# Splitting the output-projection weights on ScalarE and GpSimd, and one gating product on VectorE

## The chip, the cores and the metric

The kernel runs on one core of one Trainium2 chip. The metric is the device time of one execution in microseconds (us). A difference is measured by running the kernel before and the changed kernel on the same chip.

## What is computed

Two groups of tokens (1024 and 512, together 1536 rows of 1024 values) go through two layers that share their weights.

```python
def attn_retention_layer(x, g, w_in, qk_gain, ret_decay, w_out):
    z = rmsnorm(x, g) @ w_in
    ...
    mixed = jnp.concatenate([jax.nn.silu(ga) * oa, jax.nn.silu(gb) * ob], axis=-1)
    return x + mixed @ w_out

def windowed_layer(x, g, w_in, sink, rel_bias, w_out):
    z = rmsnorm(x, g) @ w_in
    ...
    return x + (jax.nn.silu(gate) * o) @ w_out
```

The first layer mixes tokens by dense attention (mixer A) and by retention (mixer B), the second by windowed attention (mixer C). In both, a gate multiplies the branch output, and the product goes through an output projection of 1024x1024 (w_out). A last RMSNorm follows.

## The kernel before, in words

**Products in two parts.** The matrix products run on TensorE with operands rounded to the type fp32r. To keep precision each operand is split into a high part (the rounded value) and a low part (what the rounding lost), and each product is the sum of three: high by high, low by high, high by low. For a weight tile the split is in `load_w`: a raw tile `wraw` of 128x512 (256 KB, two buffers) is fetched by a DMA on SP's queue; line 139 writes the high part on GpSimd; line 140 writes the low part, raw minus high, on GpSimd or, where the argument `lo` says so, on VectorE. The split tile `w` has four buffers. A raw buffer is free again when the low part is done, a `w` buffer when TensorE has used it.

**Tokens** are worked on in three groups t of 512 (four blocks of 128), in the order t = 2, 0, 1.

**The feature-major output projection**, `out_proj_fm`, is run for t = 2 and then t = 0 in each layer. It loops over four column chunks c; for each it calls `load_w`, which yields four `w` tiles; each tile serves 12 matmuls of 128x512 (output tile `pso`). So there are 16 `w` tiles for a group and 32 for a layer. In the first layer (weights `woab`) both parts are made on GpSimd; in the second (weights `woc`) `lo` is `nc.vector`. Line 281 adds the residual, line 283 squares the result on ScalarE, line 285 adds the square to `acc` on GpSimd.

**Where it runs.** `out_proj_fm` is a generator. Its pieces fill TensorE's queue between the pieces of attention (`pipeline`, classes `Fill` and `FillC`): while the attention of group t = 0 is computed, the projection of t = 2 runs, and so on. For t = 1 a token-major projection, `out_proj`, closes each layer; it has its own calls of `load_w`, which the change leaves alone.

**Attention around it.** Scores `s` (or `sc`) come from TensorE; VectorE reduces their maximum; ScalarE takes the exponential (line 839, or 1045) into `e` (or `ec`); GpSimd scales that by the reciprocal of the sum (line 107); TensorE transposes it to `pte`; ScalarE writes the high part `eh` (line 111) and VectorE the low part `el` (line 112); TensorE accumulates `po`. `Back.evac` adds the two halves of `po` on VectorE into `oT` (line 702).

**Gating.** For most heads `oT` is written out, and `mix_fm` later loads it with its gate, multiplies on GpSimd (line 262, tile `mo`) and splits the product into `xh` on ScalarE and `xl` on VectorE. For the last heads of groups 1 and 0 in the first layer, and of group 1 in the second, `Back.mix` does this directly: line 713 multiplies `oT` by the gate `gq` on GpSimd, and `split` makes `xh` and `xl`. That is 12 products of 128x256 in all.

**What sets the order.** Nothing is ordered by hand on an engine: the framework's scheduler (`schedule_with_timeline_sim=True`) plays the program on its own model of the engines and fixes the order of every engine's queue by it. At run time each engine works through its queue in that order and waits where an operand or a buffer isn't ready. So an instruction that moves to another engine also changes the order of the others near it.

Of the kernel before, what the change touches and what calls it, by code (L numbers as in the profile page):

```python
# [10 lines left out]
AF = mybir.ActivationFunctionType  # L11
ALU = mybir.AluOpType
# [6 lines left out]
KT = D // P  # L19
# [17 lines left out]
def trunk_kernel(ctx, tc, x, xT, wab, woab, wc, woc, gT, qkg, ret, sink, relb, fng,  # L37
                 ropeA, ropeB, dist, kdist, qdist, onehot, wmask, out_p0, out_p1, out_s):
    nc = tc.nc
# [13 lines left out]
    def buf(tag, name, n=None, dt=F32):  # L53
        t = wk.tile([P, SIZE[tag]], dt, tag=tag, name=name, bufs=BUFS[tag])
        return t if n is None else t[:, :n]

    def ps_s(name):
        return pp.tile([P, 512], F32, tag="s", name=name, bufs=5)
# [6 lines left out]
    def ps_p(name, use="fill"):  # L65
        free = ring[use]
        ring["i"] = next(i % 3 for i in range(ring["i"] + 1, ring["i"] + 4) if i % 3 in free)
        return pp.tile([P, 512], F32, tag=f"pj{ring['i']}", name=name, bufs=1)
# [58 lines left out]
        new_x(k, t)  # L127
        split(X["h", k, t], X["l", k, t], src, scale, pool)

    def load_w(arr, c, tag, lo=None, hook=None, ks=range(KT), raws=None):  # L130
        ts = {}
        for i in (k // 2 for k in ks[::2]):
            if raws is None:
                raw = wp.tile([P, 2 * CW], F32, tag="wraw", name="wraw", bufs=2)
                dma(out=raw, in_=arr[c, :, 2 * i:2 * i + 2, :].rearrange("p k n -> p (k n)"))
            else:
                raw = raws[i]
            w = wp.tile([P, 2, 2 * CW], F32R, tag=tag, name=tag, bufs=4)
            nc.gpsimd.tensor_scalar(w[:, 0, :], raw, 1.0, 1.0, ALU.mult, ALU.mult)  # L139
            (lo or nc.gpsimd).tensor_tensor(w[:, 1, :], raw, w[:, 0, :].bitcast(F32), ALU.subtract)  # L140
            ts[i] = w
            if hook is not None:
                hook(i)

        def get(s, k, a=0, n=CW):
            o = (k % 2) * CW + a
            return ts[k // 2][:, s, o:o + n]
        return get
# [18 lines left out]
    def proj_fm_k(ps, w, a, t, k, ks=range(KT)):  # L167
        mm(ps, w(0, k, a, P), X["h", k, t], k == ks[0], False)
        mm(ps, w(0, k, a, P), X["l", k, t], False, False)
        mm(ps, w(1, k, a, P), X["h", k, t], False, k == ks[-1])  # L170
# [82 lines left out]
    def stage(name):  # L253
        s = wp.tile([P, 2, 2 * CW], F32R, tag="wg", name=name, bufs=4)
        return s[:, 0, :].bitcast(F32), s[:, 1, :].bitcast(F32)
# [7 lines left out]
            split_x(o, k, t, 0.5)  # L263
            yield

    def out_proj_fm(t, warr, ks, res, dst, finish, prev, lo):
        acc = buf("T", "acc")
        for c in range(4):
            w = load_w(warr, c, "w", lo, None, ks)
            for a in range(2):  # L270
                k = 2 * c + a
                y, sq = stage("y")
                dma(out=y, in_=res(k))
                ps = ps_p("pso")
                for kk in ks:
                    proj_fm_k(ps, w, a * P, t, kk, ks)
                    if kk != ks[-1]:
                        yield
                for side in ahead[:1] + (prev or []):
                    next(side, None)  # L280
                nc.vector.tensor_tensor(y, ps, y, ALU.add)
                dma(out=dst[k][t], in_=y)
                nc.scalar.activation(sq if k else acc, y, AF.Square)
                if k:
                    nc.gpsimd.tensor_tensor(acc, acc, sq, ALU.add)
                yield
        dg, one = stage("dg")
        nc.gpsimd.memset(one[:, :P], 1.0)
        ps = ps_s("ssq")
        for j in range(GB):  # L290
            mm(ps[:, j:j + 1], acc[:, j * P:(j + 1) * P], one[:, 0:1], True, True)
        r = rstd_of(ps[:, :GB], D, GB)
        ps = ps_s("R")
        for j in range(GB):
            nc.vector.tensor_scalar(dg[:, j * P:(j + 1) * P], ident, r[:, j:j + 1], None, ALU.mult)
            mm(ps[:, j * P:(j + 1) * P], one[:, :P], dg[:, j * P:(j + 1) * P], True, True)
        rb = buf("T", "rb")
        nc.scalar.activation(rb, ps, AF.Copy)
        yield

        def fin():
            for k in range(KT):
                y = stage("yn")[0] if prev is None else buf("Q", "yn")
                dma(out=y, in_=dst[k][t])
                finish(t, k, y, rb)
                yield
        if prev is None:
            late.append(fin())
        else:
            yield from fin()  # L310

    late, ahead = [], []

    def drain(gens):
        while gens:
            for _ in gens.pop():
                pass
# [35 lines left out]
    x1T_d, x2T_d = scratch("x1T"), scratch("x2T")  # L353
# [36 lines left out]
    raws, xts = [], []  # L390
# [267 lines left out]
    for h in range(4):  # L658
        w = ws[h]
# [9 lines left out]
    class Back:  # L669
# [38 lines left out]
        def mix(self, oT):  # L708
            g = buf("Q", "gq", 256).rearrange("p (a q) -> p a q", a=2)
            sl = slice(self.j * P, (self.j + 1) * P)  # L710
            for a in range(2):
                dma(out=g[:, a, :], in_=self.gd[self.k0 + a][self.t][:, sl])
            nc.gpsimd.tensor_tensor(oT, oT, g, ALU.mult)
            for a in range(2):
                k = self.k0 + a
                if self.j == 0:
                    new_x(k, self.t)
                split(X["h", k, self.t][:, sl], X["l", k, self.t][:, sl], oT[:, a, :], 0.5)
# [140 lines left out]
    def hook_a(u):  # L859
        g, b = u  # L860
        if g == 1 and b in (BLOCKS[GB], BLOCKS[2 * GB]):
            t = 2 if b == BLOCKS[GB] else 0
            if t == 2:
                late.clear()
                fill.rest()
                fill.rate = 2.00
            drain(ahead)
            if t:
                drain([mix_fm(t, KS_A, o_ab, g_ab)])
            ahead.append(mix_fm(0 if t else 1, KS_A[:6], o_ab, g_ab))  # L870
            fill.gens.append(out_proj_fm(t, woab, KS_A, lambda k: xT[k][:, t * 512:(t + 1) * 512], x1T_d, fin_fm,
                                         None if t else late, None))

    rq1 = buf("S4", "tab").rearrange("p (f b d) -> p f b d", f=2, b=8)
    dma(out=rq1, in_=tabq_d)
# [117 lines left out]
    fillc = FillC()  # L993
# [69 lines left out]
    KS_C = tuple(range(KT))  # L1063

    def hook_c(u):
        c, b = u
        if c == 3 and b in (BLOCKS[GB], BLOCKS[2 * GB]):
            t = 2 if b == BLOCKS[GB] else 0
            for _ in fillc.gates:
                pass  # L1070
            if t == 2:
                late.clear()
            drain(ahead)
            drain([mix_fm(t, KS_C if t else KS_C[6:], o_c, g_c)])
            ahead.append(mix_fm(0 if t else 1, KS_C[:6], o_c, g_c))
            fillc.more.append(out_proj_fm(t, woc, KS_C, lambda k: x1T_d[k][t], x2T_d, fin_out, None if t else late, nc.vector))

    pipeline([(c, b) for c in range(4) for b in BLOCKS], prep_c, front_c, BUFS["E"] - 4,
             lambda kb, n: 4 if kb == n - 1 else 0, lambda n: 3.5, fillc, hook_c)
# [108 lines left out]
```

## Time and profile before

| | us |
|---|---|
| median of 3 runs (lowest to highest) | 1510.15 (1509.29 to 1511.72) |
| the profiled execution | 1511.78 |
| its span, first to last instruction | 1509.9 |
| TensorE busy in the span (PE) | 1447.9 (96%) |
| VectorE busy (DVE) | 1051.6 (70%) |
| GpSimd busy (POOL) | 810.6 (54%) |
| ScalarE busy (ACT) | 717.7 (48%) |

How to read it: PE is TensorE's matmul side and PEld its weight loads, DVE is VectorE, ACT ScalarE, POOL GpSimd, SP the engine that issues most DMAs. The busy time of an engine says how full it was over the span, not whether it held up the end. PEclk, or the granted clock, is the share of TensorE's full 2.4 GHz that it was given. In a list of instructions in order of time, a bracket tells how long the engine had stood idle before the row, and which instruction ended that wait.

### The profile page before, as it was taken

The numbers are of one execution on the slowest core, as the hardware profiler recorded it, in microseconds if no ns is written. First come the engines' busy times: TensorE is split into PE (matmuls) and PEld (weight loads), VectorE is DVE, ScalarE is ACT, GpSimd is POOL, SyncE is SP. The second block draws the span as 40 slices with busy tenths as digits, with TensorE's granted clock in tenths as the row PEclk, the third lists the DMA queues.
The fourth block names the chain that finished last, engine by engine and source line by source line (L and its number), as shares of the span: only waits on it lengthen the run. The fifth ranks groups of instructions, "written<-read, shape, count | busy, mean of one in ns | idle before, by whom it ended". The sixth has DMA issues, their size and how long they took to land.

```text
span 1509.9 us, 26043 instructions
## 1 busy us (share of the span) xinstructions
PE 1447.9 (96%) x8734; PEld 1266.1 (84%) x8734; DVE 1051.6 (70%) x2431; ACT 717.7 (48%) x1770; POOL 810.6 (54%) x1044
## 2 busy tenths in 40 slices
PE   8989999989999999989998999999999999998987
PEld 8989999977888888767777998888888888776777
DVE  7455867686676667887978237687777767889574
ACT  5632222354555555645653245566555556545102
POOL 7554654474645475887887423442622522567442
PEclk9999999999999999999999999999999999999999
DMA  9631212326212143643664231221212211567872
GB/s 327 204 122 48 77 54 71 99 74 189 74 50 66 60 117 115 208 129 108 191 211 147 78 109 45 61 77 46 75 47 87 70 46 53 168 202 274 267 235 107
DMA packets 139638, 180.79 MB, mean 120 GB/s; under 512 B 38320, under 2 KB 66992, under 8 KB 139504
## 3 DMA queue, kind: packets, MB, share of 16 engines
q1 hardware_dynamic: 137344, 173.61, 36.6%
q0 software_dynamic: 2016, 5.51, 1.3%
q8 instruction: 69, 1.13, 0.3%
q14 instruction: 65, 0.53, 0.1%
q10 hardware_dynamic: 144, 0.01, 0.0%
HBM read 127.92 MB, written 55.35 MB: 121 GB/s over the span
## 4 chain that ended last, share of the span: by engine, by line
PE 69%; DVE 10%; DMA 6%; POOL 4%; issue 4%; ACT 1%; SPq 0%; POOLq 0%; DVEq 0%; ACTq 0%
PE psg L89 17%; PE psq L89 10%; PE po L89 8%; PE psb L89 8%; PE pso L89 6%; PE pte L173 6%; PE s L89 4%; PE sc L89 3%; PE pskv L89 2%; DVE xl L118 2%; DVE w L140 1%; DVE el L112 1%; DVE nm L831 1%; DMA wraw<-in_woc 1%; PE ptq L173 1%
## 5 line engine op out<-in xcount | busy, mean ns | idle before, releaser
L89 PE MATMUL psg<-xh,wg 128*128 128x512 f32 x768 | 264.0, 401 | 0.2 <-POOL wg L140 0.2
L112 DVE TENSOR_TENSOR el<-pte,eh 128x512 fp32r<-128x512 f32 x288 | 196.4, 684 | 57.4 <-ACT eh L111 33.7
L107 POOL TENSOR_SCALAR ec<-ec,rl 128x384 f32<-128x384 f32 (+1 forms) x192 | 108.5, 578 | 233.9 <-DVE rl L1050 82.2
L111 ACT ACTIVATE eh<-pte 128x512 fp32r<-128x512 f32 x288 | 169.6, 595 | 115.0 <-PE po L89 62.9
L89 PE MATMUL pso<-xh,w 128*128 128x512 f32 x512 | 179.1, 408 | 10.5 <-POOL w L139 4.9
L89 PEld LDWEIGHTS psg<-xh,wg 128*128 128x128 f32 x768 | 143.9, 189 | 29.2 <-POOL e L107 0.9
L107 POOL TENSOR_SCALAR e<-e,rl 128x512 f32<-128x512 f32 x160 | 114.6, 727 | 91.9 <-DVE rl L842 33.9
L89 PE MATMUL psg<-xl,wg 128*128 128x512 f32 x384 | 151.0, 393 | 0.0
L1045 ACT ACTIVATE ec<-ec,nm 128x384 f32<-128x384 f32 (+1 forms) x192 | 109.5, 572 | 81.0 <-DVE nm L1043 76.0
L839 ACT ACTIVATE e<-s,nm 128x512 f32<-128x512 f32 x160 | 108.8, 686 | 70.8 <-DVE nm L836 52.5
L139 POOL TENSOR_SCALAR w<-wraw 128x512 fp32r<-128x512 f32 x116 | 80.3, 694 | 102.4 <-PE pskv L89 32.2
L831 DVE TENSOR_REDUCE nm<-s 128x1 f32<-128x512 f32 x160 | 107.7, 682 | 36.6 <-PE s L89 36.2
L89 PE MATMUL psq<-xh,w 128*128 128x512 f32 x384 | 130.0, 397 | 0.0
L89 PEld LDWEIGHTS pso<-xh,w 128*128 128x128 f32 x512 | 96.6, 191 | 34.1 <-POOL w L139 7.0
L1039 DVE CUSTOM_DVE_ANT_0 ec<-sc,bias,sink_s 128x384 f32<-128x384 f32 (+1 forms) x192 | 105.2, 568 | 21.4 <-PE sc L89 18.2
L89 PE MATMUL pso<-xl,w 128*128 128x512 f32 x256 | 102.1, 399 | 1.7 <-DVE xl L118 1.7
L173 PE MATMUL pte<-ident,e 128*128 128x128 f32 x640 | 95.5, 274 | 1.0 <-ACT e L839 0.6
L173 PEld LDWEIGHTS pte<-ident,e 128*128 128x128 f32 x640 | 78.5, 141 | 19.2 <-ACT e L839 2.2
L140 POOL TENSOR_TENSOR w<-wraw,w 128x512 fp32r<-128x512 f32 x68 | 91.4, 1347 | 1.9
L89 PEld LDWEIGHTS psg<-xl,wg 128*128 128x128 f32 x384 | 72.5, 189 | 13.1
L89 PEld LDWEIGHTS psq<-xh,w 128*128 128x128 f32 x384 | 71.9, 188 | 13.6
L173 PE MATMUL pte<-ident,ec 128*128 128x128 f32 x512 | 78.5, 273 | 1.3 <-POOL ec L107 1.1
(227 smaller groups left out, 3941.1 us busy)
## 6 DMA issues: line engine op xcount, KB each, us to landing
wraw<-in_woab SPq DMA_DIRECT2D x48, 256.0 KB, 3.4
wraw<-in_woc SPq DMA_DIRECT2D x48, 256.0 KB, 4.1
wraw<-in_wab SPq DMA_DIRECT2D x44, 256.0 KB, 3.5
wraw<-in_wc SPq DMA_DIRECT2D x36, 256.0 KB, 3.2
xt<-in_xT SPq DMA_DIRECT2D x24, 256.0 KB, 5.3
xb<-in_x SPq DMA_DIRECT2D x24, 256.0 KB, 5.1
qd<-qd SPq DMA_DIRECT2D x48, 128.0 KB, 2.9
gab<-gz SPq DMA_DIRECT2D x24, 256.0 KB, 2.0
```

The source lines that it names most:

```text
L89: i = nc.tensor.matmul(ps, lhsT=lhsT, rhs=rhs, start=start, stop=stop)
L107: nc.gpsimd.tensor_scalar(o, i, s, 1.0, ALU.mult, ALU.mult)
L111: nc.scalar.activation(hi, src, AF.Copy)
L112: nc.vector.tensor_tensor(lo, src, hi.bitcast(F32), ALU.subtract)
L118: nc.vector.scalar_tensor_tensor(lo, src, scale, hi.bitcast(F32), ALU.mult, ALU.subtract)
L139: nc.gpsimd.tensor_scalar(w[:, 0, :], raw, 1.0, 1.0, ALU.mult, ALU.mult)
L140: (lo or nc.gpsimd).tensor_tensor(w[:, 1, :], raw, w[:, 0, :].bitcast(F32), ALU.subtract)
L173: return nc.tensor.transpose(o, i, ident)
L831: nc.vector.tensor_reduce(nm2[:, c:c + 1] if nh == 2 else nm[:, h:h + 1], s, AX.X, ALU.max, negate=True)
L839: nc.scalar.activation(eh[c], ss[c], AF.Exp, bias=nm[:, h:h + 1], accum_out=l[:, h, c:c + 1])
L1039: nc.vector.tensor_tensor_reduce(es[h][:, :nk], s, bias[h][:, bo:bo + nk], 1.0, sink_s[:, 4 * c + h:4 * c + h + 1], ALU.add, ALU.max, mx[: ...
L1045: nc.scalar.activation(es[a][:, :nk], es[a][:, :nk], AF.Exp, bias=nm[:, a:a + 1], accum_out=l[:, a:a + 1])
```

## The change

In the feature-major output projection of both layers the high part of a weight tile is made by ScalarE (a copy that rounds), and the low part by GpSimd. In the second layer the low part so moves from VectorE to GpSimd; in the first it stays there. The direct gating product moves from GpSimd to VectorE. In number: 64 high parts go from GpSimd to ScalarE, 32 low parts from VectorE to GpSimd, 12 products from GpSimd to VectorE. DMAs, buffers and matmuls stay as they are.

```diff
-    def load_w(arr, c, tag, lo=None, hook=None, ks=range(KT), raws=None):
+    def load_w(arr, c, tag, lo=None, hook=None, ks=range(KT), raws=None, act=False):
...
-            nc.gpsimd.tensor_scalar(w[:, 0, :], raw, 1.0, 1.0, ALU.mult, ALU.mult)
+            if act:
+                nc.scalar.activation(w[:, 0, :], raw, AF.Copy)
+            else:
+                nc.gpsimd.tensor_scalar(w[:, 0, :], raw, 1.0, 1.0, ALU.mult, ALU.mult)
             (lo or nc.gpsimd).tensor_tensor(w[:, 1, :], raw, w[:, 0, :].bitcast(F32), ALU.subtract)
...
-    def out_proj_fm(t, warr, ks, res, dst, finish, prev, lo):
+    def out_proj_fm(t, warr, ks, res, dst, finish, prev):
...
-            w = load_w(warr, c, "w", lo, None, ks)
+            w = load_w(warr, c, "w", None, None, ks, None, True)
...
-            nc.gpsimd.tensor_tensor(oT, oT, g, ALU.mult)
+            nc.vector.tensor_tensor(oT, oT, g, ALU.mult)
...
-                                         None if t else late, None))
+                                         None if t else late))
...
-            fillc.more.append(out_proj_fm(t, woc, KS_C, lambda k: x1T_d[k][t], x2T_d, fin_out, None if t else late, nc.vector))
+            fillc.more.append(out_proj_fm(t, woc, KS_C, lambda k: x1T_d[k][t], x2T_d, fin_out, None if t else late))
```

The scheduler gives every queue a new order in two stretches, the ones in which `out_proj_fm` runs; the order elsewhere stays. (In the changed file, lines from 141 on lie three further down, and line 140 is the new ScalarE copy.)

The first place is ScalarE's queue in the first layer, around the first direct gating product (`oT_8017`; `w_83..` are weight tiles of the second chunk of t = 2, `y_8061` a residual sum). Before:

```order
L283 ACTIVATE y_8061<-y_8061 128x512
L111 ACTIVATE eh_8037<-pte_8032 128x512
L117 ACTIVATE xh50_8296<-mo_8292 128x512
L117 ACTIVATE xh20_8024<-oT_8017 128x128
L117 ACTIVATE xh30_8028<-oT_8017 128x128
L111 ACTIVATE eh_8078<-pte_8073 128x512
L839 ACTIVATE e_8109,l_7876<-s_8100,nm_7874 128x512
```

After:

```order
L117 ACTIVATE xh50_8296<-mo_8292 128x512
L140 ACTIVATE w_8330<-wraw_8328 128x512
L140 ACTIVATE w_8335<-wraw_8333 128x512
L117 ACTIVATE xh20_8024<-oT_8017 128x128
L117 ACTIVATE xh30_8028<-oT_8017 128x128
L140 ACTIVATE w_8340<-wraw_8338 128x512
L111 ACTIVATE eh_8078<-pte_8073 128x512
L286 ACTIVATE y_8196<-y_8196 128x512
L842 ACTIVATE e_8109,l_7876<-s_8100,nm_7874 128x512
```

Three high parts of weights now stand between and around the splits of the gated product, ahead of the next `eh` and exponentials.

The second place is GpSimd's queue in the second layer, in the projection of t = 0 after the last attention block (`w_1735.` and `w_1736.` are tiles of its third chunk, `acc_17134` is the running sum of squares). Before, with the low parts elsewhere:

```order
L139 TENSOR_SCALAR w_17350<-wraw_17348 128x512
L139 TENSOR_SCALAR w_17355<-wraw_17353 128x512
L139 TENSOR_SCALAR w_17360<-wraw_17358 128x512
L285 TENSOR_TENSOR acc_17134<-acc_17134,y_17278 128x512
L285 TENSOR_TENSOR acc_17134<-acc_17134,y_17313 128x512
L139 TENSOR_SCALAR w_17365<-wraw_17363 128x512
```

After, these are the low parts:

```order
L143 TENSOR_TENSOR w_17350<-wraw_17348,w_17350 128x512
L288 TENSOR_TENSOR acc_17134<-acc_17134,y_17278 128x512
L143 TENSOR_TENSOR w_17355<-wraw_17353,w_17355 128x512
L288 TENSOR_TENSOR acc_17134<-acc_17134,y_17313 128x512
L143 TENSOR_TENSOR w_17360<-wraw_17358,w_17360 128x512
L143 TENSOR_TENSOR w_17365<-wraw_17363,w_17365 128x512
```

Each of the two sums of squares now stands ahead of the next low part, where it stood behind three high parts.

## Rows read from the trace of the kernel before

**Rows 1.** Busy us by stretch: stretch, length, PE, PEld, DVE, ACT, POOL, clock, DMA share, GB/s

```profile
600.00:790.00 190.00, 179.85 (x902) 143.14 (x901) 155.80 (x286) 108.58 (x243) 157.91 (x165) 0.99 0.56 173
...
1303.00:1403.00 100.00, 89.39 (x424) 70.72 (x423) 89.85 (x198) 51.76 (x130) 73.28 (x79) 0.98 0.73 241
1403.00:1450.00 47.00, 41.13 (x172) 31.48 (x170) 25.90 (x34) 5.53 (x9) 18.05 (x21) 0.96 0.81 268
```

**Rows 2.** PE in order of time, 640 to 680 us, where it stood idle

```profile
646.29 0.50 PE L89 MATMUL po<-eh,av 128*128 128x512 f32 x1 [1.39 <-ACT eh L111]
649.19 0.50 PE L89 MATMUL s<-ak,qh 128*128 128x512 f32 x1 [2.40 <-ACT e L839]
...
674.35 0.50 PE L89 MATMUL s<-ak,qh 128*128 128x512 f32 x1 [0.82 <-ACT e L839]
```

**Rows 3.** All engines in order of time, 638 to 650 us, around the first product

```profile
638.72 0.84 DVE L702 TENSOR_TENSOR oT<-po,olo 64x256 f32<-64x256 f32 x2
...
644.49 0.72 POOL L713 TENSOR_TENSOR oT<-oT,gq 128x256 f32<-128x256 f32 x1
...
645.24 0.51 ACT L117 ACTIVATE xh<-oT 128x128 fp32r<-128x128 f32 x2 [3.77 <-POOL oT L713]
```

**Rows 4.** Busy time by stretch of 10 us after that stall

```profile
640.00:650.00 10.00, 6.20 (x26) 4.43 (x25) 6.35 (x10) 3.26 (x9) 9.90 (x11) 1.00 0.36 113
650.00:660.00 10.00, 10.00 (x48) 8.29 (x47) 7.94 (x16) 5.91 (x13) 7.44 (x9) 0.83 0.72 194
```

**Rows 5.** Waits in 600 to 790 us: total us, times, longest

```profile
ACT xh L117 <- POOL oT L713: 9.2, 5, 3.8
...
POOL w L139 <- PE pso L89: 4.4, 2, 2.5
...
POOL w L139 <- DMA wraw<-in_woab: 1.2, 2, 0.9
```

**Rows 6.** Groups of instructions of the whole span: count, busy us, mean ns

```profile
L140 POOL TENSOR_TENSOR w<-wraw,w 128x512 fp32r<-128x512 f32 x68 | 91.4, 1347 | 1.9
...
L117 ACT ACTIVATE xh<-mo 128x512 fp32r<-128x512 f32 x42 | 26.2, 627 | 37.6 <-POOL mo L262 37.5
...
L345 DVE TENSOR_TENSOR xr<-pso,xr 128x256 f32<-128x256 f32 x32 | 13.1, 416 | 22.2 <-PE pso L89 22.2
...
L713 POOL TENSOR_TENSOR oT<-oT,gq 128x256 f32<-128x256 f32 x12 | 10.2, 847 | 2.9 <-DVE oT L702 2.9
```

**Rows 7.** PE in order of time, 1310 to 1360 us, where it stood idle

```profile
1317.36 0.47 PE L89 MATMUL pso<-xh,w 128*128 128x512 f32 x1 [1.98 <-DVE oT L702]
...
1331.12 0.50 PE L89 MATMUL po<-el,cv 128*128 128x512 f32 x1 [1.12 <-DVE el L112]
...
1333.06 0.69 PE L89 MATMUL sc<-ch,qs 128*128 128x384 f32 x1 [1.09 <-DVE el L112]
...
1351.60 0.47 PE L89 MATMUL po<-eh,cv 128*128 128x512 f32 x1 [1.13 <-DVE oT L702]
```

**Rows 8.** Groups of instructions, 1303 to 1403 us

```profile
L140 DVE TENSOR_TENSOR w<-wraw,w 128x512 fp32r<-128x512 f32 x20 | 18.4, 927 | 3.3 <-POOL w L139 3.3
...
L139 POOL TENSOR_SCALAR w<-wraw 128x512 fp32r<-128x512 f32 x20 | 14.9, 746 | 4.6 <-DMA wraw<-in_woc 4.4
...
L1049 DVE TENSOR_TENSOR l<-l,se 128x2 f32<-128x2 f32 x14 | 6.6, 473 | 0.9 <-ACT se L1048 0.9
```

**Rows 9.** Groups of instructions, 1403 to 1450 us

```profile
L89 PE MATMUL pso<-xh,w 128*128 128x512 f32 x106 | 35.7, 411 | 5.6 <-POOL w L139 4.9 <-DVE w L140 0.6
...
L140 DVE TENSOR_TENSOR w<-wraw,w 128x512 fp32r<-128x512 f32 x13 | 13.2, 1016 | 17.9 <-POOL w L139 17.9
...
L139 POOL TENSOR_SCALAR w<-wraw 128x512 fp32r<-128x512 f32 x13 | 8.6, 659 | 25.3 <-DMA wraw<-in_woc 25.3
L285 POOL TENSOR_TENSOR acc<-acc,y 128x512 f32<-128x512 f32 x5 | 6.9, 1386 | 1.2 <-ACT y L283 1.2
```

**Rows 10.** DMAs of raw weight tiles, 1403 to 1450 us

```profile
DMA to landing us min/median/max: 3.4/4.4/7.1
```

## The prediction

> **What bounds the kernel now.** I read the share of busy time first, then the busy time by stretch, then, inside the stretches that the change touches, TensorE's idle times, the waits, and the groups of instructions. TensorE is busy for 1447.9 of 1509.9 us, so at most 62 us of the span is idle, and only those parts of it that lie where the projection runs can be moved. Those are three stretches: 600 to 790 us (first layer), 1303 to 1403 us (second layer, t = 2) and 1403 to 1450 us (second layer, t = 0). The reader is to subtract TensorE's busy time from each length [rows 1]: 190 - 179.85 = 10.15 us idle, 100 - 89.39 = 10.61 us, 47 - 41.13 = 5.87 us. These 26.6 us are all that the change can win, apart from the clock.
>
> Each stretch has its own limit. In the first layer the largest stall is 1.39 + 2.40 us, where TensorE waits for ScalarE's `eh` and then its exponential `e` [rows 2]. ScalarE wasn't slow: VectorE had finished `oT` at 638.72 + 0.84 = 639.56, GpSimd came to the gating product only at 644.49, and ScalarE stood idle 3.77 us in front of the split `xh` with the exponentials queued behind it [rows 3]. GpSimd was busy for 9.90 of those 10 us [rows 4]. So a GpSimd queue holds up ScalarE and through it TensorE. After the stall the granted clock was 0.83 for 10 us, between the levels 1.2 and 2.4 GHz [rows 4].
>
> In the second layer at t = 2 VectorE is the engine behind the stalls: it is busy for 89.85 of 100 us [rows 1], and the stalls of over 1 us named to it between 1310 and 1360 us are 1.98 + 1.12 + 1.09 + 1.13 = 5.32 us [rows 7]. Its instructions there contain waiting: a sum of 128x2 elements takes 473 ns, half of what a low part of 128x512 takes (927 ns) [rows 8]. At t = 0 attention is over and the weights bound: of TensorE's 5.6 us of idle time before `pso`, 4.9 us ends with GpSimd's high part, and GpSimd itself waited 25.3 us for raw tiles, so it was not full but late data was [rows 9]. A raw buffer's round is landing 4.4 us [rows 10], high part 0.66, low part 1.02 [rows 9]: 6.1 us for two tiles in two buffers.
>
> **The change part by part.** Prices: a high part on ScalarE isn't in the trace. The nearest row, ScalarE's rounding copy `xh<-mo` of the same shape, takes 627 ns; GpSimd's 659 to 746 ns bounds it from above [rows 6, 8, 9]. I take 0.63. A low part on GpSimd takes 1347 ns, against 927 and 1016 ns on VectorE [rows 6, 8, 9]. A product on VectorE isn't shown; the nearest, an addition of 128x256, takes 416 ns [rows 6], and if it has to wait out a GpSimd low part, 0.42 + 1.35 = 1.77. I take 0.42, since twelve products are few. On GpSimd it took 847 ns [rows 6]. In all GpSimd loses 64 x 0.66 + 12 x 0.85 = 52 us and gains 32 x 1.35 = 43 us; ScalarE, 48% busy, gains 64 x 0.63 = 40 us; VectorE loses 32 x 0.96 - 12 x 0.42 = 26 us. None of this is on the path by itself; the stretches decide.
>
> *First layer.* The product moves to the engine that wrote `oT`, so it can start at 639.56 rather than 644.49. The 1.39 + 2.40 us then go, and with them the reduced clock: 0.17 x 10 = 1.7 us. That makes 5.5. If the next one goes too (0.82 at 674.35 [rows 2]), 6.3. Of ScalarE's 9.2 us of waiting for products [rows 5], 3.8 is this one; the rest already cost TensorE little. Against it stand the high parts now queued on ScalarE. GpSimd waited 4.4 us for a free `w` buffer and 1.2 us for raw data [rows 5]. ScalarE now takes these waits, and behind them stand `xh`, `eh` and the exponentials that TensorE needs next, as the order of its queue around the first product shows. All of it reaching TensorE, with nothing won, would be +5.6. ScalarE's 108.58 us of work in 190 [rows 1] leaves 81 us of cover, of which about 32 x 0.63 = 20 us is filled; without that cover the 20 us would show. I take 5.5 less a quarter of the 5.6, so **-4**, between -6.3 and +5.6. Next late here is GpSimd's `mo`.
>
> *Second layer, t = 2.* VectorE loses 18.4 us of low parts and gains four products, 1.7 us: from 89.85 to 73.2 in 100 us. GpSimd, at 73.28, loses 14.9 + 4 x 0.85 and gains 20 x 1.35 = 27: 82. VectorE's slack grows from 10 to 27 us, so its queue shortens, and I take a bit over half of the 5.32 us: **-3**. At best the whole 10.6 goes; at worst the 4.4 us of waits for raw tiles [rows 8] move to ScalarE, hold its exponentials up and gain nothing: +4.4. Next late is GpSimd, whose scaling of `e` stands behind longer low parts.
>
> Why not more: VectorE's instructions wait while GpSimd works, as the 473 ns for 128x2 suggest [rows 8], and GpSimd works 27 - 18.3 = 8.7 us longer. The Trainium skill, SBUF — State Buffer, section "SBUF: two separate sides", states that VectorE operations with two SBUF inputs and GpSimd operations share a port pair under an exclusive lock, held for the whole instruction. By that rule those 8.7 us come off the 16.7 us relief, this term would be about -1.5 and the whole sum -2.5, which gives 1507.7; the slow 128x2 row agrees with it, but no row shows how much of GpSimd's added time meets such an operation.
>
> *Second layer, t = 0.* The low part that frees the raw buffer, 1.02 on VectorE, becomes 1.35: 0.33 per round, with 13 tiles in two buffers, 6.5 rounds: +2.1. The five sums `acc` of 1.39 us [rows 9] now stand directly ahead of low parts, as the order of GpSimd's queue shows; where one is met by a low part ready at that moment it delays a round, I count +0.9. So **+3**, from 0 (landings, 4.4 to 7.1, already covering the growth) to the 11 of the first rival. The high part, on ScalarE with 5.53 us of work in 47, costs nothing more; without that cover it would be 13 x 0.63 = 8 us.
>
> Matmuls and DMAs keep their number and SP's queue its order; only the time at which a raw load may be issued follows the low part. The sum is -4 - 3 + 3 = -4. The profiled execution took 1511.78, so 1507.8 by its own time; it lies 1.6 above the median of the runs, and the same -4 on the median 1510.15 gives **1506.2 us**. A measurement can tell about 0.2%, 3 us, from no change, so the forecast lies just beyond that.
>
> **Rivals.**
> 1. *GpSimd becomes the bound at t = 0: slower.* If two raw tiles land close together, their low parts queue on one engine: 0.63 + 2 x 1.35 = 3.33, and half a sum `acc` more, 0.70, before the second buffer is free. Before, with two engines, it was 2 x 0.66 + 1.02 = 2.34. That is +1.7 per round, 11 us in 6.5 rounds; with the gains of 7 halved, +7.5: 1517.6. It decides against the change once a round grows by more than 7 / 6.5 = 1.1 us. For it: this stretch has nothing else for TensorE to do. Against it: tiles that land apart never meet, and the median landing of 4.4 leaves GpSimd idle for long. The Trainium skill, GPSIMD Engine Reference, section "4.1 Engine selection", wants elementwise work with two inputs on VectorE and calls GpSimd about twice as slow; 1347 against 927 to 1016 ns is less than that here. Chance 0.22.
> 2. *ScalarE's queue blocks: slower.* The waits for raw tiles and `w` buffers (5.6 us in the first layer, 4.4 at t = 2) hold `eh` and exponentials back and cancel the gains; with t = 0 at +3 to +5 that is about +4: 1514. For it: the three high parts around the first product. Against it: ScalarE is half idle. Chance 0.10.
> 3. *The waits are only exchanged.* The product and the low parts leave, but TensorE, 96% busy, waits for the next late thing (`mo`, the reciprocal scaling) and the terms fall to -2, -2 and +3.5: -0.5, 1509.6. For it: every stall above has a second stream beside it. Against it: the 3.8 us have one clear cause. Chance 0.14.
> 4. *The stretches empty out.* Layer one gives -6.3, t = 2 gives -8 and t = 0 only +2: 1497.9. For it: two queues relieved at once. Against it: GpSimd gets more work in the second layer. Chance 0.12.
>
> **How the numbers follow.** The forecast has 0.42; its own range is 1502 to 1509, and 0.30 of it lies more than 3 us below the median, 0.12 within 3 us. Faster: 0.30 + 0.12 (rival 4) + 0.02 of rival 3 = 0.44. Same: 0.12 + 0.12 (rival 3) + 0.02 of rival 2 = 0.26. Slower: 0.22 + 0.08 = 0.30. The range of 8 in 10 reaches from rival 4 to rival 1: 1498 to 1517, leaving out half of each.
>
> **What would show it.** Right: no idle time over 1 us before `xh<-oT` on ScalarE near 640 us and no 0.83 clock after it; VectorE near 73 us in 1303 to 1403 with the 128x2 sums nearer 0.3 us; TensorE's idle time at t = 0 grown by about 3 us, ended by low parts on GpSimd. Wrong: ScalarE's copy over 0.75 us; waits of `e` or `eh` behind a weight's high part summing to over 4 us; idle time at t = 0 grown by 7 us or more, or not at all; or VectorE still behind the stalls at t = 2.

## The result, and the profile after

The changed kernel takes 1533.70 us (median of 6, 1529.95 to 1535.42) against 1510.93 us before on the same chip: a ratio of **1.0141, interval 1.0126 to 1.0156**, about 21 us slower. The forecast was 1506.2 us with a range of 1498 to 1517. Its profiled execution has a span of 1531.6 us, so 21.7 us more than the one shown of before.

To see where the time went, the same instruction is read in both traces (the last residual addition of the first layer's closing projection, the last residual sum `y` of the second layer's projection of t = 2, the last `y` of that of t = 0, the end). The lag of the changed kernel behind the one before is then, in us:

| | first layer done | t = 2 done | t = 0 done | end |
|---|---|---|---|---|
| time in the kernel before | 851.9 | 1393.6 | 1450.2 | 1509.9 |
| lag of the changed kernel | +13.9 | +15.1 | +19.2 | +21.7 |
| forecast, summed up | -4 | -7 | -4 | -4 |

So the first layer lost 14 us where 4 were to be won, t = 2 lost 1 where 3 were to be won, t = 0 lost 4 where 3 were to be lost, and 2.5 more went behind it. (The end of attention, the last `po`, would be a false mark for t = 2: in the changed kernel 12 matmuls of the projection that stood ahead of it stand behind it.) About half of the 21.7 us is not idle time: TensorE was busy for 1458.3 us instead of 1447.9 with as many matmuls, at a mean granted clock of 0.984 instead of 0.992.

Busy time by stretch after the change (columns as in [rows 1]; the stretches are those of before, moved by the lag):

```profile
600.00:804.00 204.00, 183.56 (x892) 145.29 (x891) 157.99 (x293) 124.39 (x274) 137.55 (x132) 0.96 0.52 160
650.00:660.00 10.00, 7.31 (x28) 5.75 (x29) 7.23 (x18) 7.65 (x18) 7.34 (x8) 0.66 0.57 177
1317.00:1416.00 99.00, 88.69 (x412) 70.93 (x412) 82.39 (x179) 61.72 (x149) 77.33 (x74) 0.95 0.72 234
1416.00:1470.00 54.00, 45.57 (x182) 32.89 (x182) 19.21 (x26) 14.13 (x25) 29.61 (x25) 0.97 0.81 262
```

In the first layer TensorE's idle time doubled, from 10.15 to 20.4 us, though GpSimd is emptier (137.55 in 204 us, against 157.91 in 190) and VectorE no fuller. At t = 0 it rose from 5.87 to 8.4 us. The three longest stalls of the first layer, TensorE in order of time:

```profile
652.69 0.79 PE L89 MATMUL po<-eh,av 128*128 128x512 f32 x1 [5.27 <-ACT eh L111]
...
707.72 0.66 PE L176 MATMUL ptq<-ident,qd 128*128 128x128 f32 x4 [2.20 <-ACT e L842]
...
759.78 0.79 PE L89 MATMUL s<-ak,qh 128*128 128x512 f32 x1 [4.38 <-ACT e L842]
```

The first one stands where the 1.39 + 2.40 us of [rows 2] stood, and it has grown. ScalarE and VectorE ahead of it:

```profile
640.78 0.63 ACT L117 ACTIVATE xh<-mo 128x512 fp32r<-128x512 f32 x1 [6.72 <-POOL mo L265]
...
645.27 0.84 DVE L705 TENSOR_TENSOR oT<-po,olo 64x256 f32<-64x256 f32 x2
...
646.77 1.50 DVE L716 TENSOR_TENSOR oT<-oT,gq 128x256 f32<-128x256 f32 x1
...
648.30 0.51 ACT L117 ACTIVATE xh<-oT 128x128 fp32r<-128x128 f32 x2 [1.88 <-DVE oT L716]
651.39 0.63 ACT L140 ACTIVATE w<-wraw 128x512 fp32r<-128x512 f32 x1 [2.58 <-DMA wraw<-in_woab]
652.04 0.60 ACT L111 ACTIVATE eh<-pte 128x512 fp32r<-128x512 f32 x1
```

The reader is to see three waits in one queue. ScalarE waits 6.72 us for GpSimd's `mo`, with `eh`, the exponentials and `olo` behind it, so VectorE writes the sum that the product takes only at 645.27 (638.72 before). Then ScalarE waits for the product, which is done at 648.27, 2.2 us after that sum: it does follow its sum quickly, but the sum is late. Then it waits 2.58 us for a raw tile, with the next `eh` behind. The granted clock of 0.66 in the next 10 us, between its levels of 1.2 and 2.4 GHz, adds to it; there it was 0.83 before [rows 4].

The third stall comes from VectorE. GpSimd works without a pause, and VectorE's instructions stretch:

```profile
754.56 1.80 POOL L143 TENSOR_TENSOR w<-wraw,w 128x512 fp32r<-128x512 f32 x1
756.32 1.30 POOL L857 TENSOR_TENSOR yn<-yn,rb 128x512 f32<-128x512 f32 x1
757.59 1.31 POOL L143 TENSOR_TENSOR w<-wraw,w 128x512 fp32r<-128x512 f32 x1
```

```profile
755.16 2.62 DVE L118 SCALAR_TENSOR_TENSOR xl<-oT,xh 128x128 fp32r<-128x128 f32 x2
757.70 1.21 DVE L839 TENSOR_TENSOR nm<-nm 128x1 f32<-128x1 f32 x1
```

An operation on 128x1 elements took 1.21 us, and the exponential behind it started at 758.95. (The second stall, 2.20 us, is left open.)

The prices of the weight parts were right. Groups of 600 to 804 us, then of 1416 to 1470 us:

```profile
L143 POOL TENSOR_TENSOR w<-wraw,w 128x512 fp32r<-128x512 f32 x28 | 38.1, 1368 | 10.6 <-ACT w L140 10.6
...
L140 ACT ACTIVATE w<-wraw 128x512 fp32r<-128x512 f32 x28 | 17.5, 630 | 9.6 <-DMA wraw<-in_woab 8.7 <-issue 1.0
...
L716 DVE TENSOR_TENSOR oT<-oT,gq 128x256 f32<-128x256 f32 x6 | 6.4, 1072 | 0.1
...
L143 POOL TENSOR_TENSOR w<-wraw,w 128x512 fp32r<-128x512 f32 x13 | 18.1, 1397 | 19.2 <-ACT w L140 19.0
L140 ACT ACTIVATE w<-wraw 128x512 fp32r<-128x512 f32 x13 | 8.2, 630 | 28.6 <-DMA wraw<-in_woc 28.6
```

A high part costs 0.63 us on ScalarE as forecast, a low part 1.37 to 1.40 on GpSimd (1.35). The product, 1.07 against 0.42, lies midway between its bounds of 0.42 and 1.77. At t = 0 GpSimd isn't full: it waits 19.0 us for ScalarE, and ScalarE 28.6 us for raw tiles.

### The profile page after: what moved, and what is told of

It is laid out like the page before. It is cut to its first block, busy times and chain, and to the rows that moved or that the text cites. A ratio compares the mean times of both kernels' runs of the same rounds, so it can differ in the third digit from the quotient of the medians.

```text
span 1531.6 us, 26082 instructions
## 1 busy us (share of the span) xinstructions
PE 1458.3 (95%) x8734; PEld 1273.0 (83%) x8734; DVE 1039.8 (68%) x2411; ACT 752.0 (49%) x1834; POOL 802.4 (52%) x1000
## 4 chain that ended last, share of the span: by engine, by line
PE 70%; DVE 8%; DMA 7%; POOL 3%; issue 3%; ACT 3%; SPq 1%; POOLq 0%; DVEq 0%; ACTq 0%
PE psg L89 17%; PE psq L89 10%; PE po L89 8%; PE psb L89 8%; PE pso L89 8%; PE pte L176 7%; PE s L89 4%; PE sc L89 3%; PE pskv L89 2%; DVE xl L118 2%; DMA wraw<-in_woab 1%; PE ptq L176 1%; DMA wraw<-in_woc 1%; DMA yn<-x2T 1%; ACT e L842 1%
## 5 line engine op out<-in xcount | busy, mean ns | idle before, releaser
L89 PE MATMUL pso<-xh,w 128*128 128x512 f32 x512 | 185.6, 418 | 10.6 <-ACT w L140 6.2
L143 POOL TENSOR_TENSOR w<-wraw,w 128x512 fp32r<-128x512 f32 x100 | 134.8, 1353 | 37.7 <-ACT w L140 33.6
L176 PEld LDWEIGHTS pte<-ident,ec 128*128 128x128 f32 x512 | 64.3, 142 | 15.4 <-issue 0.9
```

Source lines behind the costliest of these rows:

```text
L89: i = nc.tensor.matmul(ps, lhsT=lhsT, rhs=rhs, start=start, stop=stop)
L176: return nc.tensor.transpose(o, i, ident)
```

## The experiments

Four theories stand against each other. **1:** ScalarE's high parts wait for raw tiles and hold `eh` and the exponentials behind them. **2:** the product on VectorE is late. **3:** low parts on GpSimd free the raw buffers late. **4**, formed after the first runs: the scheduler's new order of all queues makes the loss. Ratios are against runs of the kernel before on the same chip, with 95% intervals; 0.1% is 1.5 us. All kernels are edits of the kernel before by this hook, with `hi` set for a layer at the call:

```diff
-            nc.gpsimd.tensor_scalar(w[:, 0, :], raw, 1.0, 1.0, ALU.mult, ALU.mult)
+            if hi is None:
+                nc.gpsimd.tensor_scalar(w[:, 0, :], raw, 1.0, 1.0, ALU.mult, ALU.mult)
+            elif hi is nc.scalar:
+                nc.scalar.activation(w[:, 0, :], raw, AF.Copy)
...
```

### The parts one by one

Product alone:

```diff
-            nc.gpsimd.tensor_tensor(oT, oT, g, ALU.mult)
+            nc.vector.tensor_tensor(oT, oT, g, ALU.mult)
```

> Only the twelve gating products move to VectorE; high and low parts of weights stay where they were before. Theory 1 (ScalarE's high parts wait for raw tiles and hold eh and the exponentials behind them, which costs the 14 us in the first layer): the product alone is harmless, -4 to +1 us. Theory 2 (the product on VectorE, 1.07 us each in the changed kernel instead of 0.42, makes VectorE late): +5 to +10 us, of it most between 600 and 800 us.

Measured: 1.0020 [1.0008, 1.0032], 3 us, between what the two theories had.

First layer's high parts alone:

```diff
-                                         None if t else late, None))
+                                         None if t else late, None, nc.scalar))
```

> Only the 32 high parts of the first layer move to ScalarE; products stay on GpSimd, the second layer stays as before. Theory 1: +8 to +14 us, all before 820 us, with ScalarE waiting over 6 us for raw tiles in that stretch. Theory 2: within 4 us of before.

Measured: 1.0050 [1.0031, 1.0068]. Theory 1's sign, just under its size.

Second layer alone, high parts to ScalarE and low parts to GpSimd:

```diff
-            fillc.more.append(out_proj_fm(t, woc, KS_C, lambda k: x1T_d[k][t], x2T_d, fin_out, None if t else late, nc.vector))
+            fillc.more.append(out_proj_fm(t, woc, KS_C, lambda k: x1T_d[k][t], x2T_d, fin_out, None if t else late, None, nc.scalar))
```

> Only the second layer changes: 32 high parts to ScalarE, 32 low parts to GpSimd; products stay on GpSimd. Theory 1: the stretch of t = 0 costs +6 to +8 us by itself, since raw buffers come free later, and t = 2 gives 0 to -2: +5 to +8 us in all. Theory 2: the second layer is worse only through its four products, so 0 to +3 us here.

Measured: 1.0095 [1.0068, 1.0121], 14 us, about twice what theory 1 had.

Both edits together, no product:

> The whole change without its product part: products stay on GpSimd. Theory 1: close to the changed kernel, +18 to +24 us against before, about the sum of the two runs on one layer. Theory 2: well under the changed kernel, +5 to +12 us.

Measured: 1.0125 [1.0091, 1.0158], 19 us, as theory 1 had it. The parts alone add up to 0.20 + 0.50 + 0.95 = 1.65% against the 1.41% of the change, which their intervals don't tell apart.

### Waiting, raw buffers and low parts

ScalarE only touches each raw tile:

```diff
+            if touch:
+                nc.scalar.activation(w[:, 1, 0:1], raw[:, 0:1], AF.Copy)
...
```

> The kernel before, except that ScalarE copies one column of each of the 64 raw weight tiles of the projection into the tile's low half, which the low part then overwrites: about 0.2 us of work each, 13 us over the whole span on an engine that is half idle, but ScalarE now has to wait for each raw tile in its queue. High and low parts stay where they were. Theory 1 (ScalarE's queue standing in front of late raw tiles is the cost): +8 to +18 us, with ScalarE waiting over 30 us for raw tiles. Theory 3 (the cost is the work moved and the later low parts): within 4 us of before.

Measured: 1.0021 [1.0007, 1.0035]. Its touches, groups of 600 to 804 and of 1303 to 1460 us:

```profile
L140 ACT ACTIVATE w<-wraw 128x1 fp32r<-128x1 f32 x28 | 5.6, 202 | 6.7 <-DMA wraw<-in_woab 4.0 <-issue 1.8 <-PE pso L89 0.9
...
L140 ACT ACTIVATE w<-wraw 128x1 fp32r<-128x1 f32 x32 | 6.3, 199 | 42.4 <-DMA wraw<-in_woc 41.1 <-DMA x2T<-y 1.3
```

ScalarE waited 45 us for raw tiles, as theory 1 wanted, and the kernel lost 3. So waiting in that queue is not dear by itself, and theory 1 falls as the main cause in the second layer. In the first layer ScalarE waited only 4.0 us here, against 8.7 in the changed kernel, so this run doesn't decide there; the run in the old order below does.

Three raw buffers, with the change and without:

```diff
-                raw = wp.tile([P, 2 * CW], F32, tag="wraw", name="wraw", bufs=2)
+                raw = wp.tile([P, 2 * CW], F32, tag="wraw", name="wraw", bufs=3)
...
-    BUFS = dict(E=12, S4=3, S2=3, H=4, Q=8, T=2, O=2)
+    BUFS = dict(E=12, S4=3, S2=3, H=4, Q=7, T=2, O=2)
```

> The changed kernel with three raw buffers instead of two (room for it comes from the work pool Q, seven buffers instead of eight, in this run and the next). Theory 1: with a raw tile in hand earlier ScalarE hardly waits, so the loss mostly goes: within 6 us of the next run. Theory 3: 14 to 22 us above the next run, as the changed kernel stands to the one before.

> The kernel before with three raw buffers and seven buffers in pool Q, the control of the run above. Both theories: -5 to +2 us against before; a gain would come from 1403 to 1450 us, where GpSimd waits 25 us for raw tiles.

Measured: 1.0043 [1.0027, 1.0058] with the change and 0.9989 [0.9973, 1.0005] without. More than half of the loss goes with a third buffer, which the kernel before hardly needs: the changed one is more exposed to the raw round. But the scheduler orders these anew as well, so this doesn't separate the theories.

Second layer with high parts on ScalarE, low parts left on VectorE:

```diff
-            fillc.more.append(out_proj_fm(t, woc, KS_C, lambda k: x1T_d[k][t], x2T_d, fin_out, None if t else late, nc.vector))
+            fillc.more.append(out_proj_fm(t, woc, KS_C, lambda k: x1T_d[k][t], x2T_d, fin_out, None if t else late, nc.vector, nc.scalar))
```

> Second layer only: high parts on ScalarE, low parts left on VectorE, products on GpSimd. Against the run with low parts on GpSimd (+13 us) it tells the slow low part from the waiting of ScalarE. Theory 1: still +7 to +14 us. Theory 3 (raw buffers freed late by GpSimd's low part): 0 to +4 us.

Measured: **0.9938 [0.9924, 0.9953]**, 9 us faster than before, and better than any theory had it. This is the faster version of the next runs. Its edit differs from that of the run of 1.0095 only in the engine of the low parts, though the scheduler's order differs too.

The low parts alone (`lo` from `nc.vector` to None):

> Second layer only: the 32 low parts move from VectorE to GpSimd, the high parts stay on GpSimd. Nothing new stands on ScalarE. Theory 3 (the low part on GpSimd frees the raw buffer late, and the projection of t = 0 waits for raw tiles): +10 to +20 us, most of it between 1400 and 1475 us. Theory 1 (ScalarE's waiting): within 4 us of before.

Measured: 1.0075 [1.0058, 1.0092], 11 us: what theory 3 had for the second layer, and where it had it. In its profile the lag is 0.8 us at the end of t = 2 and 12.1 at the end of t = 0.

The changed kernel with that part undone:

> The changed kernel with one part undone: the second layer's low parts go back to VectorE. By the runs on the second layer alone (1.0095 with low parts on GpSimd, 0.9938 on VectorE) theory 3 expects about 22 us less than the changed kernel, so -4 to +4 us against before, with what is left of the loss before 860 us. Theory 1 expects most of the 21 us to stay, +12 or more.

Measured: 1.0027 [1.0013, 1.0041], 1.1% or 17 us better than the changed kernel, but not the full 22.

First layer with high parts on ScalarE and low parts on VectorE:

> First layer only: high parts to ScalarE, and low parts from GpSimd to VectorE, products on GpSimd. If the +7.5 us of the run with high parts alone come from a low part that GpSimd starts late (theory 3), the raw buffer now comes free sooner: -4 to +3 us. If ScalarE's work and waits ahead of eh and the exponentials are the cost there (theory 1), +5 to +10 us again. VectorE, 82 percent busy there, is the risk of this run: then over +10.

Measured: 1.0053 [1.0035, 1.0070], as with the low parts on GpSimd (1.0050). So in the first layer the low part's engine makes no difference that these runs show.

The faster version with three raw buffers:

> The faster version found so far (second layer: high parts on ScalarE, low parts on VectorE) with three raw buffers and pool Q at seven. If the raw round still bounds the projection of t = 0, -12 to -16 us against before; if it no longer does, -7 to -11 as without the third buffer.

Measured: 0.9958 [0.9943, 0.9973]: the third buffer adds nothing there.

The faster version with the first layer's low parts on VectorE:

> The faster version (second layer: high parts on ScalarE, low parts on VectorE) with the first layer's low parts on VectorE too, its high parts left on GpSimd. If GpSimd's queue is what holds ScalarE up in the first layer, -11 to -15 us against before; if VectorE becomes late there, -4 us or worse.

Measured: 1.0035 [1.0022, 1.0048]. VectorE, or the order that came with it, can't take them.

### Engines and order apart

In all these runs the scheduler was free to order the queues anew. Between the kernel before and the changed one 1295 of TensorE's 8497 matmuls stand at another place in the queue, and of the instructions that stay on their engine 332 of VectorE's (its custom operations not counted), 243 of SP's, 183 of ScalarE's and 141 of GpSimd's. The next kernels hold every queue to a given order, by dependencies between neighbours on the same engine that order and don't synchronise; a moved instruction stands where it was dispatched in that order. The numbers that are unpacked are those of the instructions in the order of another kernel. (In the profiles of these kernels `xh` is line 119, `eh` 113, `e` 846, the product 720, a high part 142 on GpSimd and 144 on ScalarE, a low part 147.)

```diff
         trunk_kernel(tc, *args)
...
+        byname = {i.name: i for i in nc.main_func.blocks[1].instructions}
...
+        for d in struct.unpack(f"<{len(raw) // 4}i", raw):
+            n += d
+            i = byname.get(f"I-{n}")
...
+            if i.engine in last:
+                tc.add_manual_dep(i, last[i.engine], info, reason="the order of the kernel before")
+            last[i.engine] = i.name
```

First layer's high parts, old order:

> First layer's high parts on ScalarE, as in the run that gave 1.005, but with every engine's queue held to the order of the kernel before by order-only dependencies; a high part stands in ScalarE's queue at the point at which it was dispatched before. Theory 4 (the scheduler's new order is the cost in the first layer, not the engine): -3 to +2 us. Theory 1 (ScalarE's work and its waits ahead of eh and the exponentials): +5 to +10 us, as with the new order.

Measured: 1.0000 [0.9982, 1.0018], where the new order gave 1.0050. ScalarE waited 6.7 us for raw tiles in 600 to 790 us here, more than the 5.6 of the forecast, and its work and waits cost nothing; neither does holding the queues.

Product, old order:

> Only the twelve products on VectorE, every queue in the order of the kernel before. Theory 4: the product alone gains now, -4 to 0 us, since the wait of 3.8 us near 640 us goes and nothing else moves. If VectorE's product is itself the cost (it took 1.07 us in the changed kernel, waiting for GpSimd inside it): +2 to +5 us, as with the new order (1.002).

Measured: 0.9983 [0.9970, 0.9997], a small gain, where the new order gave 1.0020. VectorE, ScalarE and TensorE at the place of [rows 2, 3], and the 10 us after it:

```profile
641.53 0.74 DVE L720 TENSOR_TENSOR oT<-oT,gq 128x256 f32<-128x256 f32 x1
```

```profile
642.56 0.50 ACT L119 ACTIVATE xh<-oT 128x128 fp32r<-128x128 f32 x2
...
647.35 0.69 ACT L846 ACTIVATE e<-s,nm 128x512 f32<-128x512 f32 x1 [2.72 <-DVE nm L843]
```

```profile
648.18 0.51 PE L91 MATMUL s<-ak,qh 128*128 128x512 f32 x1 [1.63 <-ACT e L846]
```

```profile
650.00:660.00 10.00, 9.90 (x52) 7.85 (x50) 8.10 (x14) 5.15 (x11) 9.60 (x11) 1.00 0.71 199
```

The split follows the product at once, the stall of 1.39 us is gone, and the clock stays at 1.00: the forecast's picture, in the order that it was read in. But the stall of 2.40 us is still 1.63, and the exponential waits for VectorE's `nm`. It did so in the kernel before, too:

```profile
645.58 1.61 DVE L118 SCALAR_TENSOR_TENSOR xl<-oT,xh 128x128 fp32r<-128x128 f32 x2 [2.19 <-ACT xh L117]
647.12 1.21 DVE L836 TENSOR_TENSOR nm<-nm 128x1 f32<-128x1 f32 x1
```

```profile
648.36 0.69 ACT L839 ACTIVATE e<-s,nm 128x512 f32<-128x512 f32 x1 [2.13 <-DVE nm L836]
```

The late product was only the first part of that wait; the rest is VectorE's slow `xl` and `nm`, which the move leaves.

The whole change, old order:

> The whole change with every queue in the order of the kernel before. Theory 3 (low parts of the second layer on GpSimd free the raw buffers late): still +10 to +18 us, most of it after 1400 us. Theory 4 (the new order made the loss): -5 to +5 us.

Measured: **1.0014 [0.9998, 1.0031]**, against 1.0141 with the new order. Theory 4 has most of the loss; what theory 3 had for this run, 10 to 18 us, did not come.

The kernel before, no part moved, in the order of the changed kernel:

> The kernel before with every engine's queue held to the order of the changed kernel: no part moves to another engine. Theory 4 (the order makes the loss): +12 to +22 us. If order and engines only hurt together: -4 to +6 us.

Measured: **1.0209 [1.0184, 1.0233]**. The order alone loses 31 us, more than theory 4 had; in it the moved parts win back a third (1.0141).

The faster version, old order:

> The faster version (second layer: high parts on ScalarE, low parts on VectorE; 0.994) with every queue in the order of the kernel before. If its gain is the engine's: -6 to -12 us against before, most of it after 1300 us. If its gain too was the new order: -3 to +3 us.

Measured: 0.9941 [0.9921, 0.9961], against 0.9938 in the scheduler's own order. Its gain is the engine's and stays.

The lags behind the kernel before, as in the first table, in us:

| | first layer done | t = 2 done | t = 0 done | end |
|---|---|---|---|---|
| before, new order | +19.2 | +25.1 | +30.8 | +31.0 |
| whole change, old order | -2.2 | +3.6 | +5.6 | +5.5 |
| faster version, old order | -0.3 | -4.8 | -8.8 | -8.6 |

These are single executions; the kernels' first attention instructions differ by up to 0.8 us already, and the one of the whole change (1517.2 us) lies 2.1 us above the median of its runs (1515.14).

**How an order costs.** The kernel before in the new order, ScalarE, then GpSimd, then TensorE:

```profile
756.15 0.51 ACT L119 ACTIVATE xh<-oT 128x128 fp32r<-128x128 f32 x2 [5.99 <-POOL oT L720]
756.68 0.60 ACT L113 ACTIVATE eh<-pte 128x512 fp32r<-128x512 f32 x1
```

```profile
750.71 1.05 POOL L142 TENSOR_SCALAR w<-wraw 128x512 fp32r<-128x512 f32 x1
751.74 1.26 POOL L147 TENSOR_TENSOR w<-wraw,w 128x512 fp32r<-128x512 f32 x1
752.96 1.26 POOL L861 TENSOR_TENSOR yn<-yn,rb 128x512 f32<-128x512 f32 x1
754.17 1.26 POOL L147 TENSOR_TENSOR w<-wraw,w 128x512 fp32r<-128x512 f32 x1
755.39 0.72 POOL L720 TENSOR_TENSOR oT<-oT,gq 128x256 f32<-128x256 f32 x1
```

```profile
757.33 0.80 PE L91 MATMUL po<-eh,av 128*128 128x512 f32 x1 [6.90 <-ACT eh L113]
```

The same place in the kernel before, ScalarE:

```profile
744.93 0.63 ACT L117 ACTIVATE xh<-mo 128x512 fp32r<-128x512 f32 x1 [0.59 <-POOL mo L262]
745.47 0.58 ACT L111 ACTIVATE eh<-pte 128x512 fp32r<-128x512 f32 x1
745.95 0.68 ACT L839 ACTIVATE e<-s,nm 128x512 f32<-128x512 f32 x1
...
746.61 0.51 ACT L117 ACTIVATE xh<-oT 128x128 fp32r<-128x128 f32 x2
```

In the old order `eh` and an exponential stood ahead of the split `xh<-oT`, and ran while the product was made; in the new order the split stands ahead of them, and they wait 5.99 us with it. In the changed kernel VectorE made this product earlier and ScalarE didn't wait for it here; there the waits fell elsewhere, as at 648.30 and 651.39 above.

**How the low part costs.** The whole change in the old order, TensorE, ScalarE and GpSimd in the second layer:

```profile
1385.39 1.22 PE L91 MATMUL pso<-xh,w 128*128 128x512 f32 x2 [4.75 <-POOL w L147]
```

```profile
1379.72 0.63 ACT L144 ACTIVATE w<-wraw 128x512 fp32r<-128x512 f32 x1 [4.31 <-DMA wraw<-in_woc]
```

```profile
1381.26 1.47 POOL L269 TENSOR_TENSOR mo<-mo 128x512 f32<-128x512 f32 x1 [5.40 <-DMA mo<-gc]
1382.69 1.38 POOL L292 TENSOR_TENSOR acc<-acc,y 128x512 f32<-128x512 f32 x1
1384.03 2.55 POOL L147 TENSOR_TENSOR w<-wraw,w 128x512 fp32r<-128x512 f32 x2
```

The high part was ready at 1380.35. GpSimd, idle for 5.40 us, stood in front of `mo` waiting for its gate, then did `mo` and `acc`; the low part came 3.7 us late. GpSimd was not full (75.74 of the 100 us): it was in line behind the wrong thing. TensorE's waits of this kind in 1303 to 1403 us (total us, times, longest), first in the kernel before, where VectorE makes the low parts, then in the whole change in the old order:

```profile
PE pso L89 <- DVE w L140: 2.3, 2, 1.6
```

```profile
PE pso L91 <- POOL w L147: 9.7, 3, 4.8
```

In the faster version in the old order, with the low parts on VectorE, they are 2.4 us, the longest 1.7.

## Why the prediction was wrong

By the runs in the old order the change splits into: first layer's high parts 0.00%, products -0.17%, second layer's high parts -0.59%, and by difference its low parts about 0.14 + 0.17 + 0.59 = +0.90% (14 us); the rest, 1.41 - 0.14 = 1.27% (19 us), is the new order. The difference carries the uncertainty of four ratios, about 0.3%, and takes it for granted that the parts add up, which no run shows.

- **What bounds the kernel:** the first layer's stall at 646 us had the cause that was named, and in the old order it goes as forecast, clock included; but all twelve products together win 2.6 us. VectorE's queue as the cause of the stalls at t = 2 was named rightly for two of the four, as the third point shows. What the forecast did not see is that the second layer gains without relief for VectorE. The faster version in the old order, t = 2 (columns as in [rows 1]):

```profile
1303.00:1403.00 100.00, 91.14 (x444) 73.35 (x444) 89.03 (x204) 62.91 (x152) 60.21 (x60) 1.00 0.76 250
```

VectorE is as full as before (89.03 and 89.85), GpSimd has gone from 73.28 to 60.21 without the high parts, and t = 2 takes 4.5 us less. The forecast had no term for the high parts' leaving GpSimd.
- **First layer, -4:** measured +13.9 by the lag. The step that failed is "I take 5.5 less a quarter of the 5.6": it let an instruction move with its own price and with the waits read in the old order, up to +5.6, and held the rest of the queues still. With the rest held still the lag is -2.2; in the new order, with no part moved, it is +19.2. Two places of the new order stood ahead of the forecast, but the whole shift, 1295 matmuls of TensorE among it, had no term and no rival. "SP's queue its order" was wrong as well: 243 of its instructions moved. And in the old order 5.5 was too much for the product: 1.39 us went, 2.40 became 1.63, and the clock gave 1.7, together 3.9.
- **Second layer, t = 2, -3:** measured +1.2 by the lag (15.1 - 13.9), and +5.8 in the old order (3.6 + 2.2). The step "VectorE's slack grows from 10 to 27 us, so its queue shortens" held there: of the four stalls of [rows 7] the two that `oT` ended are gone, and the other two remain. The whole change in the old order, TensorE, then the stretch:

```profile
1329.16 0.49 PE L91 MATMUL po<-el,cv 128*128 128x512 f32 x1 [1.18 <-DVE el L114]
...
1330.86 0.44 PE L91 MATMUL sc<-ch,qs 128*128 128x384 f32 x1 [0.85 <-DVE el L114]
```

```profile
1303.00:1403.00 100.00, 86.49 (x391) 69.50 (x390) 76.79 (x170) 59.17 (x142) 75.74 (x73) 0.91 0.71 225
```

So 5.32 us became 2.03, the 3 us that were forecast. VectorE fell to 76.79 us, not to 73.2, in the direction of the forecast's paragraph on why not more. What failed is a term put at nothing: "Next late is GpSimd" gave no price to TensorE's waiting for a low part that stands in GpSimd's queue behind `mo` and `acc`. These waits are 9.7 us where they were 2.3, and the clock of the stretch is 0.91 where it was 0.98.
- **Second layer, t = 0, +3:** measured +4.1 (19.2 - 15.1) and +2.0 in the old order (5.6 - 3.6), inside the 0 to 11 given. The sign that was named for it did not come: in the changed kernel ScalarE's high part ends 6.2 us of TensorE's waits there, GpSimd's low part 1.4. A later free raw buffer can still be behind the late high parts, and the third buffer's help agrees with it, but the order is in this number too; how much of the hit is luck stays open.
- **Rivals:** the first had the right sign and engine, 1517.6 against 1533.7. Its mechanism, two low parts queueing at t = 0 with half a sum between, isn't what the stall shown last has: that one is at t = 2, and `mo`, its DMA and a whole sum stand ahead. The page it cited, the Trainium skill, GPSIMD Engine Reference, section "4.1 Engine selection", advises VectorE for such work. The runs with the low parts side by side agree in direction (0.9938 and 1.0095). The second rival, ScalarE's queue, is half right: splits and weights do stand ahead of `eh`, but the old order shows that the high parts alone don't cost it. The third, waits only exchanged, is what the old order shows in the second layer: VectorE's waits go and GpSimd's come (1.0014 in all). The fourth did not come.
- **Signs that were named:** ScalarE's copy stayed under 0.75 us; ScalarE stood idle 1.88 us before `xh<-oT`, not under 1; the clock after 650 us fell to 0.66 and didn't stay full; VectorE took 82.39 us at t = 2, not near 73, and the sums of 128x2 453 ns, not 300; TensorE's idle time at t = 0 grew by 2.5 us.

What stays open: which of the moved instructions in the new order carries how much of the 31 us, beyond the places shown; why the scheduler's model preferred that order; and the low parts alone in the old order. None was tried.

## What to carry to other kernels

Where a scheduler orders the queues, moving an instruction to another engine is two changes, and the second can be the larger: compare the orders on all engines, and hold the old one to time the move by itself. An engine with idle time is no free place for a step that others wait for, since in an in-order queue it waits behind whatever late thing stands ahead, as the low parts did on GpSimd. Idle time is not the whole loss: of the 21.7 us here, 10.4 are TensorE being busy for longer, at a lower granted clock. The version to keep here is the second layer's high parts on ScalarE with the low parts on VectorE, 0.9938 of the time before.

## What was not expected of the hardware

While GpSimd works without a pause, a small VectorE operation can take as long as one of GpSimd's: 1.21 us for 128x1 at 757.70, 2.62 us for two splits of 128x128. The whole trace of the changed kernel shows it as well. The 31 `nm` operations of 128x1 that ran while GpSimd stood idle took 144 to 161 ns; the 30 that ran wholly beside GpSimd's work took 142 to 1294 ns. In the kernel before it is 148 to 160 ns (23) and 142 to 1286 ns (35). The product took 1072 ns on VectorE in the changed kernel, 788 ns alone in the old order and 517 ns in the whole change in the old order (means of the first layer):

```profile
L720 DVE TENSOR_TENSOR oT<-oT,gq 128x256 f32<-128x256 f32 x7 | 3.6, 517 | 0.2
```

So the price of a VectorE operation is not fixed: it goes with what GpSimd does beside it. The Trainium skill, SBUF — State Buffer, section "SBUF: two separate sides", describes an exclusive lock on a port pair that the two share. These rows agree with it, and no run here isolates it.
